# Ragged self-attention on one core: value products moved behind the last projection in four positions, counters raised ahead in the 256 loop, one score group in other banks

## The chip, the cores and the metric

The kernel runs on 1 core of one Trainium2 chip. The metric is the device time of one execution in microseconds (us), as the median of several runs. Its engines are TensorE (PE in the profile, PEld for its weight loads), VectorE (DVE), ScalarE (ACT), GpSimd (POOL) and SyncE (SP), which here issues nearly all DMAs.

## What is computed

Self-attention with 8 heads of 64 over 32 sequences of different lengths, without an output projection. The lengths are drawn once, between 64 and 511; rows beyond a sequence's length are zero in the output.

```python
for b in range(batch):
    x_b = x[b, :seq_len].copy()
    qkv = np.matmul(x_b, w_qkv)
    q, k, v = np.split(qkv, 3, axis=-1)
    ...
    scores = scale * np.matmul(q, k.transpose(0, 2, 1))
    attn = np.exp(scores - scores_max)
    attn = attn / (np.sum(attn, axis=-1, keepdims=True) + 1e-08)
    out_b = np.matmul(attn, v).transpose(1, 0, 2).reshape(seq_len, dim)
    output[b, :seq_len] = out_b
```

## The kernel before

**Loops and positions.** The kernel sorts the sequences by length on the chip and takes them in 16 pairs, longest first. There is one hardware loop for each width N in `LOOPS` (512, 448, 384, 352, 320, ... 96); a pair runs in the narrowest loop that holds its longer sequence. With this draw the last loops run as follows: 288 once, 256 once, 224 twice, 192 once, 160 twice, 128 once, 96 once. Each pass of a loop has two positions, j = 0 and j = 1. Position j computes the attention of the pair's sequence j, and between these steps the projections (queries, keys, values) of the sequence that comes next.

**The order of work** within a position is written out by hand as a string per loop, `ORDER`, one half for each position. A step is a letter and a number, and behind @ stand the PSUM banks (of 8) that it uses:

- `S` a group of scores, with its exponentials on ScalarE (line 1298). TensorE line 1280.
- `B`, `U`, `V..a` projections (queries and keys; values) made of 64-row matmuls in two or three parts a, b, c that share two banks (line 1334). Letters behind the colon tell which engine copies the banks out, d for VectorE and a for ScalarE.
- `Q`, `K`, `V` the same as full 128-row matmuls in one bank (lines 303 and 314); * means copied by ScalarE, else by VectorE.
- `A` value products: exponentials times values. `A0@3` is line 1528 with 128 rows (`av`); `A0a@23 ... A0b` come in two parts of 64 rows (`paired`, line 1642).
- `Z` the products with the last half tile of keys, 64 rows (`rest`, line 1568). In the loops where the last tile is at most half full (here 192 and 160, among others), the normalisation of two A steps follows only behind their Z.
- `W`, `E` smaller projection steps; `L`, `P` masks on VectorE and the cast of the next x on GpSimd.
- `D` and `X`: SyncE loads a later x, and transposes the cast x by DMA into `xT`, which the projections of the same position in the next pass read. X may only overwrite `xT` when the last projection of its position has read it.

**Normalisation.** Behind A (or Z), VectorE does three instructions for each A step: the row sums times a mask (`U`, line 1743, or 1704 for a paired A), the reciprocal (`R`, 1739 or 1695) and the division out of PSUM into the output tile (`O`, 1677). Only after `O` is the bank free. Each engine runs its instructions strictly in the order in which the steps stand. In P, VectorE's mask for the next cast stands behind the divisions of the position before.

**Waits.** `plan_waits` works out from the data and the banks which step waits for which; a wait is a semaphore against a counter register. These registers are raised once per pass (`raise_all`). On TensorE `LATE` says how many of its last steps of a pass stand behind the raising, with their waits corrected for it; the raising and the branch run on TensorE's sequencer while queued matmuls still run. Without an entry, the raising comes last.

**SyncE** goes through X, D and the store of the output (ST, once all `O` of the position are done) in that order, position by position.

The diff touches only `LATE` (line 41) and four entries of `ORDER` (lines 265 to 279), and with them what `position` (line 1038 on) emits in which order.

Of the kernel before, what the change touches and what calls it, by code (L numbers as in the profile page):

```python
# [18 lines left out]
P = 128  # L19
# [18 lines left out]
    passed: object = None  # L38


LATE = {288: 3, 224: 3, 192: 1, 160: 3}


def plan_waits(head, bodies, entries, rare):
# [136 lines left out]
def kernel(  # L181
# [9 lines left out]
    B, MAXS, D = x.shape  # L191
# [15 lines left out]
    def ring(n, shape, dtype, name, pool=const):  # L207
# [74 lines left out]
    }  # L282
# [1714 lines left out]
    for v, N in enumerate(LOOPS):  # L1997
        mine = [k for k, op in enumerate(bodies[v][1]) if op.eng == "PE"]
        tails_of.append(mine[len(mine) - LATE.get(N, 0) :])
        assert not any(bodies[v][1][k].skip for k in tails_of[v])  # L2000
# [242 lines left out]
```

## Time and profile before

| | us |
|---|---|
| median of 3 runs (lowest to highest) | 325.65 (325.38 to 325.74) |
| the profiled execution | 326.82 |
| its span, first to last instruction | 325.0 |
| TensorE busy in the span | 311.3 |
| ScalarE, VectorE, GpSimd busy | 264.0, 193.4, 100.6 |

The granted TensorE clock is 0.993 of full speed in the mean. The positions that the change touches lie in the last third of the span. By the starts of TensorE's first score group: 288 loop, position 0 at 209.80; 256 loop at 230.78, its position 1 at 237.99; 224 loop at 244.9 (with a projection); 192 loop at 272.98, position 1 at 278.46; 160 loop, first pass at 285.10 and 290.74, second pass at 296.49 and 301.37; 128 loop at 307.42.

How to read the lines: in a timeline a line is start in us, duration in us, engine, line of the program, operation, what is written and read, the shape, how many instructions were merged, and in brackets how long the engine was idle before it and what released it. TensorE's matmuls overlap and their ends are modelled, so the distance of two starts says more than a duration. In the chain of waits a line is start, duration and what the end of the span waited for.

### The profile page before, as it was taken

How to read it: one execution, taken by the hardware profiler on the slowest of the kernel's cores; microseconds unless marked ns; L12 is line 12 of the kernel's file. 1: busy time of each engine (PE TensorE's matmuls, PEld its weight loads, DVE VectorE, ACT ScalarE, POOL GpSimd, SP SyncE). 2: the span in 40 equal slices, each digit the busy share in tenths (PEclk: the TensorE clock that was granted, in tenths of full speed). 3: DMA queues.
4: the chain of work that ended last, by engine and by line, in shares of the span. 5: the costliest groups of instructions: out<-in, count | busy, mean ns of one | idle time of the engine just before them, and what ended most of it. 6: DMA issues, size and time to landing. Idle time of an engine off the chain costs nothing.

```text
span 325.0 us, 13310 instructions
## 1 busy us (share of the span) xinstructions
PE 311.3 (96%) x5092; PEld 202.2 (62%) x5092; DVE 193.4 (60%) x650; ACT 264.0 (81%) x415; POOL 100.6 (31%) x147
## 2 busy tenths in 40 slices
PE   7999999999999999999999999999999899999991
PEld 4444645555656556556556657657787787877861
DVE  6866566566665546456456456436575666666753
ACT  4489899797878988988988979898877678777761
POOL 2657040414030330330330342143222223533420
PEclk9999999999999999999999999999999999999997
DMA  6986858497848999597677777756459957896652
GB/s 216 373 316 72 259 180 277 94 351 171 281 50 281 224 294 261 185 285 226 227 225 226 244 210 198 221 169 219 135 150 206 233 179 178 180 239 161 216 180 81
DMA packets 69448, 68.85 MB, mean 212 GB/s; under 512 B 40720, under 2 KB 40720, under 8 KB 69392
## 3 DMA queue, kind: packets, MB, share of 16 engines
q1 hardware_dynamic: 69344, 68.12, 74.8%
q8 instruction: 33, 0.54, 0.7%
q14 instruction: 23, 0.19, 0.2%
q10 hardware_dynamic: 48, 0.00, 0.0%
HBM read 25.17 MB, written 33.55 MB: 181 GB/s over the span
## 4 chain that ended last, share of the span: by engine, by line
PE 88%; DMA 4%; DVE 2%; issue 1%; ACT 1%; SPq 1%; POOL 0%; POOLq 0%; DVEq 0%
PE banks L1334 43%; PE banks L1280 14%; PE banks L1528 12%; PE banks L314 7%; PE banks L303 6%; DMA xT<-x 3%; PE banks L1642 3%; PE banks L1221 1%; PE banks L1568 1%; DMA x_nat<-in_x_dram 1%; DVE out_nat L1677 0%; PE banks L768 0%; ACT et L1298 0%; SPq L331 0%; ACT xT L777 0%
## 5 line engine op out<-in xcount | busy, mean ns | idle before, releaser
L1298 ACT ACTIVATE et<-banks 128x704 f16<-128x704 f32 (+8 forms) x256 | 199.1, 825 | 25.8 <-PE banks L1280 22.0
L374 POOL TENSOR_TENSOR x<-x_nat,mask 128x512 f16<-128x512 f32 x82 | 83.1, 1039 | 177.1 <-DVE mask L1062 170.0
L1334 PE MATMUL banks<-xT,w_r 64*128 64x352 f16 (+9 forms) x1536 | 127.7, 294 | 1.4 <-DMA xT<-x 1.0
L1334 PEld LDWEIGHTS banks<-xT,w_r 64*128 64x128 f16 x1536 | 68.9, 94 | 37.8 <-PE banks L1334 8.7
L1280 PE MATMUL banks<-qz,kT 64*128 64x352 f16 (+11 forms) x624 | 77.4, 294 | 1.3 <-ACT et L1298 0.4
L1677 DVE SCALAR_TENSOR_TENSOR out_nat<-rcp,banks 128x256 f32<-128x256 f32 (+1 forms) x128 | 59.4, 470 | 6.5 <-DMA out_dram<-out_nat 2.2
L1378 DVE CAST qz<-banks 128x448 f16<-128x448 f32 (+6 forms) x47 | 26.4, 562 | 46.6 <-PE banks L1334 45.8
L1528 PEld LDWEIGHTS banks<-v_aug,et 128*128 128x128 f16 x1248 | 42.0, 97 | 14.4 <-issue 7.2
L1528 PE MATMUL banks<-v_aug,et 128*128 128x65 f16 x1248 | 47.6, 194 | 0.7 <-ACT et L1298 0.6
L1334 PE MATMUL banks<-w_r,xT 64*128 64x512 f16 (+1 forms) x368 | 46.6, 372 | 0.3 <-ACT v_aug L1500 0.3
L1280 PEld LDWEIGHTS banks<-qz,kT 64*128 64x128 f16 x624 | 28.0, 94 | 24.0 <-issue 5.9
L1743 DVE TENSOR_TENSOR rcp<-banks,queries 128x4 f32<-128x4 f32 (+1 forms) x110 | 17.3, 157 | 19.8 <-PE banks L1528 7.3
L1397 DVE CAST v_aug<-banks 128x512 f16<-128x512 f32 x25 | 16.6, 690 | 19.2 <-PE banks L1334 19.2
L314 PE MATMUL banks<-w_r,xT 128*128 128x512 f16 x104 | 26.7, 380 | 0.0
L1334 PEld LDWEIGHTS banks<-w_r,xT 64*128 64x128 f16 x368 | 17.1, 94 | 14.5 <-PE banks L1334 1.0
L303 PE MATMUL banks<-xT,w_r 128*128 128x160 f16 (+3 forms) x256 | 23.2, 243 | 1.1 <-issue 0.6
L1378 ACT CAST kT<-banks 128x352 f16<-128x352 f32 (+6 forms) x47 | 22.5, 479 | 1.5 <-PE banks L1334 1.5
L1739 DVE RECIPROCAL rcp<-rcp 128x4 f32<-128x4 f32 (+1 forms) x110 | 20.2, 184 | 3.8
L1378 DVE CAST kT<-banks 128x352 f16<-128x352 f32 (+5 forms) x33 | 17.9, 552 | 7.7 <-PE banks L1334 7.6
L303 PEld LDWEIGHTS banks<-xT,w_r 128*128 128x128 f16 x256 | 16.5, 98 | 6.2 <-issue 1.2
L1378 ACT CAST qz<-banks 128x352 f16<-128x352 f32 (+6 forms) x33 | 15.3, 464 | 3.4 <-PE banks L1334 3.3
L1500 ACT CAST v_aug<-banks 128x512 f16<-128x512 f32 x15 | 8.9, 590 | 9.5 <-PE banks L314 9.5
(117 smaller groups left out, 180.4 us busy)
## 6 DMA issues: line engine op xcount, KB each, us to landing
x_nat<-in_x_dram SPq DMA_DIRECT2D x12, 768.0 KB, 6.7
out_dram<-out_nat SPq DMA_DIRECT2D x12, 768.0 KB, 4.1
x_nat<-in_x_dram SPq DMA_DIRECT2D x14, 512.0 KB, 4.6
out_dram<-zeros SPq DMA_DIRECT2D x12, 512.0 KB, 3.7
out_dram<-out_nat SPq DMA_DIRECT2D x12, 512.0 KB, 5.1
out_dram<-out_nat SPq DMA_DIRECT2D x4, 1024.0 KB, 6.8
x_nat<-in_x_dram SPq DMA_DIRECT2D x3, 1024.0 KB, 7.0
out_dram<-zeros SPq DMA_DIRECT2D x4, 768.0 KB, 4.5
```

The source lines that it names most:

```text
L303: last = nc.tensor.matmul(dst[:, 0:N], w_r[:, c, w0 : w0 + P], xT[:, c, 0:N], start=(c == 0), stop=(c == NC - 1),)
L314: last = nc.tensor.matmul(pv, xT[:, c, t * P : (t + 1) * P], w_r[:, c, 2 * D : 3 * D], start=(c == 0), stop=(c == NC - 1),)
L374: return engine.tensor_tensor(out=x16, in0=x32, in1=live.broadcast_to([P, D]), op=ALU.mult)
L1280: last = nc.tensor.matmul(psc[par][:, x * wide : x * wide + N], kT[r, i, c0 : c0 + P], qz[r, i, 0:N], start=True, stop=True,)
L1298: return nc.scalar.activation(out=et[:, :, x0:x1, 0:N], in_=got.rearrange("p j (x q) -> p j x q", q=wide)[:, :, x0:x1, 0:N], func=AF.Exp, ...
L1334: last = nc.tensor.matmul(to, lhs(rows, c), rhs(rows, c), start=(c == 0 and opens), stop=(c == NC - 1 and not opens),)
L1378: return lambda copy, bank: copy(out=buf[:, ms, 0:M], in_=bank[:, 0 : gm * M].rearrange("p (m q) -> p m q", q=M),)
L1397: return lambda copy, bank: copy(out=v_bufs[o][:, t, :, 0:HD], in_=bank.rearrange("p (h d) -> p h d", d=HD))
L1528: last = nc.tensor.matmul(pav[:, g, qt, :], e_bufs[e][:, c0 + qt * P : c0 + (qt + 1) * P], v_aug[:, kt, h, :], start=(kt == 0 and not (hal ...
L1677: return nc.vector.scalar_tensor_tensor(out=o_t[:, 0:n, h0 * HD : (h0 + heads) * HD].rearrange("p t (g d) -> p t g d", d=HD), in0=by, scal ...
L1739: return nc.vector.reciprocal(out=r, in_=total if n == 1 else r)
L1743: return nc.vector.tensor_tensor(out=r.rearrange("p (t g) -> p t g", t=n), in0=total.rearrange("p (t g) -> p t g", t=n), in1=rows, op=ALU. ...
```

## The change

- **288, position 0:** the score group S3 uses banks 6 and 7 instead of 5 and 6.
- **256, position 1:** A0b and B1b change places, and A4 and A6 move from ahead of B1c, the last projection part, to the end. `LATE` gets an entry 256: 2, so TensorE raises its counters ahead of these two.
- **192, position 1:** V0a moves ahead of A1a, and A1b from ahead of V0b to the end. `LATE` was 1 and stays 1, so the step behind the raising is now A1b instead of V0b.
- **160, both positions:** A2 and Z0 move behind the last projection (Q2 in position 0, V0 in position 1), to stand ahead of A4, A6 and Z4.

X and D keep their place among SyncE's steps; they now stand ahead of the moved value products in the string. The number of instructions of each kind stays the same.

```diff
-LATE = {288: 3, 224: 3, 192: 1, 160: 3}
+LATE = {288: 3, 256: 2, 224: 3, 192: 1, 160: 3}
...
-        288: "L P D S0@56 B2a@24 S5@01 B2b:aa S3@56 B0a@01 S1@23 S9@45 B0b:dd S2@67 B1a@32 S6@45 B1b:da S4@67 "
+        288: "L P D S0@56 B2a@24 S5@01 B2b:aa S3@67 B0a@01 S1@23 S9@45 B0b:dd S2@67 B1a@32 S6@45 B1b:da S4@67 "
...
         256: "L P S0@34 U0a@02 S1@56 U0b:aa B0a@17 S2@34 S3@56 B0b A0a@02 B0c:da B1a@34 A0b B1b A1a@67 B1c:ad X D "
-        "A1b | L P S0@01 U0a@25 S1@34 U0b:ad B0a@76 S2@01 E0@4 B0b A0a@23 B0c:da B1a@45 S3@01 A0b B1b A4@6 "
-        "A6@7 B1c:aa X D",
+        "A1b | L P S0@01 U0a@25 S1@34 U0b:ad B0a@76 S2@01 E0@4 B0b A0a@23 B0c:da B1a@45 S3@01 B1b A0b B1c:aa "
+        "X D A4@6 A6@7",
...
         192: "L P S0@01 S1@23 V0*@5 B0a@40 S3@67 B0b A0a@53 S2@12 A0b B1a@67 B0c:aa B1b A1a@21 B1c:ad X D A1b | L "
-        "P B0a@50 S1@34 B0b S2@67 B0c:da W0@4 S0@12 B1a@03 S3@67 E0@5 B1b A0a@12 B1c:aa A0b A1a@46 V0a@57 A1b "
-        "V0b:aa X D",
-        160: "L P S0@01 S1@23 V0@5 Q0*@4 A0@0 K0*@7 A2@1 S2@23 Z0 K2*@6 Q2*@7 X D A4@5 A6@2 Z4 | L P S0@34 S1@67 "
-        "K2@0 Q2*@1 A0@3 W0*@4 Q0@6 A2@5 K0*@0 Z0 S2@12 V0*@6 X D A4@4 A6@7 Z4",
+        "P B0a@50 S1@34 B0b S2@67 B0c:da W0@4 S0@12 B1a@03 S3@67 E0@5 B1b A0a@12 B1c:aa A0b V0a@57 A1a@46 "
+        "V0b:aa X D A1b",
+        160: "L P S0@01 S1@23 V0@5 Q0*@4 A0@0 K0*@7 S2@23 K2*@6 Q2*@7 X D A2@1 Z0 A4@5 A6@2 Z4 | L P S0@34 S1@67 "
+        "K2@0 Q2*@1 A0@3 W0*@4 Q0@6 K0*@0 S2@12 V0*@6 X D A2@5 Z0 A4@4 A6@7 Z4",
```

The unchanged entries of the two loops that follow are needed to see who uses which bank next: 224 begins `L P B0a@30 S0@12`, and 128 begins `L P S0@12 Q0*@6 K0*@0 V0@7`.

## The prediction

> **What bounds the kernel now.** I read the page first, for who ends the span, then the timeline of TensorE around the five changed positions, then VectorE, ScalarE and SyncE at those places, and the chain of waits.
>
> ```profile
> PE 88%; DMA 4%; DVE 2%; issue 1%; ACT 1%; SPq 1%; POOL 0%; POOLq 0%; DVEq 0%
> ```
>
> TensorE carries 88% of the chain that ended last. So an edit pays only where it closes a gap in TensorE's row, and costs where it opens one. I call the four runs of the 160 loop P0 (first pass, position 0), P1 (first pass, position 1), P2 and P3 (second pass); the 128 loop follows.
>
> ```profile
> 287.08 0.29 PE L1528 MATMUL banks<-v_aug,et 128*128 128x65 f16 x4
> 287.20 0.71 PE L303 MATMUL banks<-xT,w_r 128*128 128x160 f16 x8
> 287.76 0.28 PE L1528 MATMUL banks<-v_aug,et 128*128 128x65 f16 x4
> 287.97 0.31 PE L1280 MATMUL banks<-qz,kT 64*128 64x160 f16 x4
> 288.12 0.28 PE L1568 MATMUL banks<-v_aug,et 64*128 64x65 f16 x8
> 288.34 1.07 PE L303 MATMUL banks<-xT,w_r 128*128 128x160 f16 x13
> 290.06 0.37 PE L303 MATMUL banks<-xT,w_r 128*128 128x160 f16 x3 [0.65 <-issue]
> ...
> 290.74 0.58 PE L1280 MATMUL banks<-qz,kT 64*128 64x160 f16 x12
> 291.26 1.28 PE L303 MATMUL banks<-xT,w_r 128*128 128x160 f16 x16
> 292.38 0.29 PE L1528 MATMUL banks<-v_aug,et 128*128 128x65 f16 x4
> ...
> 294.05 0.72 PE L303 MATMUL banks<-xT,w_r 128*128 128x160 f16 x8
> 294.70 0.30 PE L1568 MATMUL banks<-v_aug,et 64*128 64x65 f16 x8
> 294.83 0.30 PE L1280 MATMUL banks<-qz,kT 64*128 64x160 f16 x4
> ...
> 295.94 0.41 PE L1528 MATMUL banks<-v_aug,et 128*128 128x65 f16 x8
> ...
> 296.49 0.62 PE L1280 MATMUL banks<-qz,kT 64*128 64x160 f16 x12
> 297.09 1.04 PE L314 MATMUL banks<-w_r,xT 128*128 128x512 f16 x4
> ...
> 306.57 0.41 PE L1528 MATMUL banks<-v_aug,et 128*128 128x65 f16 x8
> 306.92 0.30 PE L1568 MATMUL banks<-v_aug,et 64*128 64x65 f16 x8
> 307.42 0.40 PE L1280 MATMUL banks<-qz,kT 64*128 64x128 f16 x8 [0.20 <-ACT v_aug L1500]
> ...
> 309.54 1.03 PE L314 MATMUL banks<-w_r,xT 128*128 128x512 f16 x4
> ...
> 311.63 1.53 PE L303 MATMUL banks<-xT,w_r 128*128 128x96 f16 x32 [0.48 <-DMA xT<-x]
> ```
>
> Starts tell more than durations here, since the ends are modelled. In P0, A0 (287.08, four matmuls) is followed by 128-row work and takes 0.12 us from start to start; A2 (287.76), the same four matmuls, takes 0.21 because the 64-row S2 follows. So a change between 128-row and 64-row matmuls costs 0.09 us. A half product Z0 takes 0.13 where 64-row work follows (294.70 to 294.83) and 0.22 where it doesn't (288.12 to 288.34): the same 0.09.
>
> ```profile
> 292.18 0.42 DVE L1677 SCALAR_TENSOR_TENSOR out_nat<-rcp,banks 128x256 f32<-128x256 f32 x1
> ...
> 292.81 0.48 DVE L1453 CAST kT<-banks 128x320 f16<-128x320 f32 x1
> ...
> 295.04 0.16 DVE L1743 TENSOR_TENSOR rcp<-banks,queries 128x4 f32<-128x4 f32 x1 [0.42 <-PE banks L1568]
> ...
> 295.87 0.42 DVE L1677 SCALAR_TENSOR_TENSOR out_nat<-rcp,banks 128x256 f32<-128x256 f32 x1 [0.46 <-DMA out_dram<-out_nat]
> 296.21 0.15 DVE L1743 TENSOR_TENSOR rcp<-banks,queries 128x4 f32<-128x4 f32 x1
> ...
> 296.61 0.42 DVE L1677 SCALAR_TENSOR_TENSOR out_nat<-rcp,banks 128x256 f32<-128x256 f32 x1
> ```
>
> This is VectorE behind P0 and P1. P1's four divisions start only after Z0: the first link of the chain begins at 295.04, 0.21 after Z0's work. A link that isn't held up takes 0.82 from its begin to the end of its division (296.21 to 297.03), and divisions follow 0.74 apart (295.87, 296.61). These divisions release PSUM banks. The second, O2, holds bank 5 and ends at 297.03; the next position's V0@5 starts at 297.09. That is no accident: P2's V0 waits for it already.
>
> **The change, part by part.** *160.* A2 and Z0 go behind the last projection in all four runs. That removes no work. It adds two row changes per run (Z0 now lies between 128-row products), 0.19 us, and starts the division chain later, while the next position wants the banks as early as before.
>
> P0: the gap before 290.06 has no releaser, so I take it for code arriving. It comes after 65 matmuls of the loop; in the new order these end inside Z0. The work before it stays nearly the same, so I keep its end at 290.06. Three matmuls of Z0 (0.05), a row change, A4 and A6 (0.25, twice four as above), another change and Z4 (0.13) end P0 at 290.67, 0.07 before 290.74. Bound: with the gap gone altogether, 0.6 less.
>
> P1: P0's Z0 ends at 290.11, the chain begins at 290.32, O0 ends 291.14, O2 291.88, O6 293.36. K2@0 needs O0's bank and comes at 291.19, just in time. Q2@1 comes 0.56 later (half of 291.26 to 292.38) and needs O2: it waits 0.18, to 291.94. K2's copy, behind O6 on VectorE, ended 0.69 after it (293.29 against 292.60), so now at 294.05; K0@0 needs that bank, comes at 294.04 (294.05 − 0.07 + 0.18 − 0.12 for A2) and waits 0.06. With the row changes P2 starts 0.36 late (0.19 + 0.24 − 0.07), at 296.85.
>
> P2: P1's V0 no longer has A2 and Z0 ahead, so it ends at 295.94 + 0.17 − 0.25 = 295.86, and Z0 behind A2 and a row change at 296.20. The chain begins at 296.41: O0 ends 297.23, O2 297.97. S1@23, 0.21 behind S0, needs bank 3 from O0 and waits 0.2, to 297.29. V0@5 then comes at 297.59 and waits for O2 until 298.03. It started at 297.09, so P2 is 0.94 late at V0, and 1.13 at its end.
>
> P3: P1's waits recur (0.24), with two row changes, so Z4, which ended at 307.05 (306.92 and 0.13), ends at 307.05 + 1.56 = 308.61. Here the change pays: the 128 loop's first scores started at 307.42, 0.37 behind Z4, because they wait for ScalarE's copy of V0, 0.85 behind V0's end at 306.57. V0 now ends at 306.57 + 1.13 + 0.24 − 0.25 = 307.69, so the scores start at about 308.65, 1.23 late. V0@7 of the 128 loop would come at 309.54 + 1.23 = 310.77, but P3's last division holds bank 7: Z0 ends 308.03, the chain begins 308.24 and its fourth division ends 3.04 later, 311.28. V0@7 waits 0.57 and is 1.80 late. Then the 0.48 of wait for transposed x at 311.63 falls away: 1.32 late.
>
> ```profile
> 291.58 3.97 SPq L331 DMA_TRANSPOSE xT<-x  x2
> ...
> 297.99 1.26 SPq L331 DMA_TRANSPOSE xT<-x  x1
> ```
> ```profile
> 306.86 4.51 DMA xT<-x
> ```
>
> Are the transposes sooner, as the order allows? P0's last projection ended three matmuls behind 290.06 and P1's at 295.94, but SyncE reached their transposes at 291.58 and 297.99: its own queue of loads and stores holds them, not TensorE. P3's, at 306.86, does follow its projection; that now ends at 307.69, so it goes out at 308.0, and with the old 4.51 it lands at 312.5, before its reader at 312.95. SyncE's store behind P3 waits for the late O6 (311.28) and holds back the 128 loop's own transpose; its reader has moved 1.3 too, so I price that from 0 to 0.3 and take 0.1. GpSimd's casts wait for a mask that VectorE makes behind the divisions; they move along, hidden as long as SyncE comes later still.
>
> The row change is weighed once more. The rows say 0.09 each. The Trainium skill ("TensorE: Matmul & The Clock Gate", Part 3, the mechanism) says that a weight load to other rows, or to the background buffer, is pulled ahead of running matmuls, by which a change would be free and the sum 0.3 less; the trace speaks against that here.
>
> *256.*
>
> ```profile
> 242.79 0.41 PE L1642 MATMUL banks<-v_aug,et 64*128 64x65 f16 x16
> ...
> 244.48 1.05 PE L1334 MATMUL banks<-xT,w_r 64*128 64x224 f16 x16
> ...
> 252.82 0.56 PE L1334 MATMUL banks<-xT,w_r 64*128 64x224 f16 x8 [0.96 <-DMA xT<-x]
> ```
> ```profile
> 243.68 0.75 DVE L1677 SCALAR_TENSOR_TENSOR out_nat<-rcp,banks 128x256 f32<-128x256 f32 x2
> ```
> ```profile
> 246.43 6.25 DMA xT<-x
> ```
>
> A4 and A6 go behind the last projection part, A0b behind B1b, about 0.8 later (sixteen matmuls, as many as the row at 244.48). A0b's division ended at 244.43; it will end at 245.2, and the next loop's first projection, the second half of that row and so due at 244.9, needs its bank: 0.3 late. Raising the counters ahead hides a loop end that can't be longer than a small part of that row. Both lie ahead of the 0.96 of wait at 252.82, which swallows them. What counts is when that transpose lands. It goes out some 0.6 earlier, but it took 6.25 on the chain against 4.51 above, so it stands in the queue. I take its landing as unchanged, 0; ends 0.6 earlier and 0.1 later.
>
> *192 and 288.*
>
> ```profile
> 284.46 0.61 PE L1334 MATMUL banks<-w_r,xT 64*128 64x256 f16 x8
> 285.10 0.62 PE L1280 MATMUL banks<-qz,kT 64*128 64x160 f16 x12
> ```
> ```profile
> 212.99 0.30 PE L1280 MATMUL banks<-qz,kT 64*128 64x288 f16 x2 [0.36 <-ACT et L1298]
> ```
> ```profile
> 212.25 2.95 ACT L1298 ACTIVATE et<-banks 128x576 f16<-128x576 f32 x5
> ```
>
> In 192, V0a moves ahead of A1a, and A1b goes last. A short stall ahead of V0b can close, since A1a's sixteen products now cover V0a's drain where A1b's eight did. But V0b's start (284.46) lies 0.64 before the next loop (285.10), 0.2 more than its eight matmuls fill, so TensorE already waits there for the branch; the branch comes behind A1b now, a third as long a cover. What the one gives the other takes: 0, ends −0.1 and +0.1. In 288, S3 leaves bank 5, so S9@45 waits no longer for S3's exponential but for a copy that ends before it. The 0.36 goes, yet ScalarE's five exponentials run without a break and the second is awaited soon after. I take 0.15 off; ends 0 and 0.36.
>
> **Sum.** 1.32 + 0.1 − 0.15 = 1.27 on a profiled execution of 326.82 us (span 325.0): 328.1. That execution lies 1.17 above the median of 325.65, so the forecast is 326.9.
>
> **Rivals.** *Transposes win (faster).* If the later divisions hold nobody up, because the waits in the 160 loop ask for an earlier count than I read, P1 to P3 cost only row changes (0.5 at Z4, with P0's gain); the 0.37 before 307.42 pays most of that, and the wait at 311.63 the rest. If then the 256 transpose lands 0.6 earlier and 288 gives 0.15, the kernel is 0.75 faster: 324.9. It decides at P2's V0, which must start without a wait for VectorE. Against it: V0 starts 0.06 behind O2 in the trace. *Offset (no change).* The gap in P0 goes (−0.6) and the 256 transpose lands 0.6 earlier, with the chain as forecast: +0.07, 325.7. *The gap grows.* Code arrives 0.6 later in P0: 327.5.
>
> **How the numbers follow.** About 0.65 us (0.2%) is what can be told from no change. Chances: forecast within its bounds 0.66, gap grows 0.06, offset 0.16, transposes win 0.12. The forecast's own range is 326.2 to 327.4. The range for 8 in 10 adds the larger gap and most of the offset case: 325.4 to 327.6.
>
> **What would show it.** Right: two more row changes in each run of 160; P2's S1 and V0 and the 128 loop's V0 waiting for VectorE's divisions; the waits at 307.42 and 311.63 gone; the start at 252.82 within 0.2. Wrong: P2 as long as before, or the start at 252.82 moved by 0.5.

## The result, and the profile after

The changed kernel takes 329.02 us in the median of nine runs (327.86 to 329.93), the kernel before 326.0 (325.38 to 328.08). The ratio is 1.0082, with a 95% interval of 1.0059 to 1.0105: 1.9 to 3.4 us slower, 2.7 by the ratio itself. The forecast was 1.27 slower, so the sign was right and the size was less than half; the time lies above the range given for 8 in 10 (325.4 to 327.6). The profiled execution of the changed kernel took 329.93, with a span of 328.1.

By engine, the chain that ended last in the changed kernel:

```profile
PE 87%; DVE 5%; issue 2%; DMA 2%; ACT 1%; SPq 1%; POOL 0%; DVEq 0%; POOLq 0%
```

VectorE has gone from 2% to 5%: its divisions now stand on the path. TensorE's timeline in the 160 loop and behind it, changed kernel (P0's end, the start of P2, then the 128 loop):

```profile
289.85 1.28 PE L303 MATMUL banks<-xT,w_r 128*128 128x160 f16 x16
290.96 0.29 PE L1528 MATMUL banks<-v_aug,et 128*128 128x65 f16 x4
291.18 0.30 PE L1568 MATMUL banks<-v_aug,et 64*128 64x65 f16 x8
291.41 0.42 PE L1528 MATMUL banks<-v_aug,et 128*128 128x65 f16 x8
...
298.06 0.86 PE L1280 MATMUL banks<-qz,kT 64*128 64x160 f16 x12
299.29 1.04 PE L314 MATMUL banks<-w_r,xT 128*128 128x512 f16 x4 [0.36 <-DVE out_nat L1677]
...
310.01 0.40 PE L1280 MATMUL banks<-qz,kT 64*128 64x128 f16 x8
310.34 1.96 PE L303 MATMUL banks<-xT,w_r 128*128 128x128 f16 x32
312.73 1.02 PE L314 MATMUL banks<-w_r,xT 128*128 128x512 f16 x4 [0.43 <-DVE out_nat L1677]
313.59 0.42 PE L1528 MATMUL banks<-v_aug,et 128*128 128x65 f16 x8
313.95 0.40 PE L1280 MATMUL banks<-qz,kT 64*128 64x128 f16 x8
314.81 0.38 PE L303 MATMUL banks<-xT,w_r 128*128 128x96 f16 x5 [0.46 <-DVE v_aug L1500]
```

The order is the one described: projections (289.85), then A2, Z0, A4 and A6. The wait ahead of the 128 loop's first scores, at 307.42 before, is gone at 310.01, as forecast. P2's V0 (299.29) now starts 1.23 behind its first scores (298.06) and names VectorE's division as releaser; before, the distance was 0.60. The 128 loop's V0 (312.73) waits for the same line. The last row is the one to remember: 0.86 lie between the scores and the projection behind them, as before (310.76 to 311.63 there), but the releaser is another one. VectorE at that place, changed kernel:

```profile
309.54 0.16 DVE L1743 TENSOR_TENSOR rcp<-banks,queries 128x4 f32<-128x4 f32 x1 [1.69 <-PE banks L1568]
...
312.17 0.42 DVE L1677 SCALAR_TENSOR_TENSOR out_nat<-rcp,banks 128x256 f32<-128x256 f32 x1
...
313.80 0.69 DVE L1500 CAST v_aug<-banks 128x512 f16<-128x512 f32 x1 [0.33 <-PE banks L314]
```

P3's four divisions run from 309.54 to 312.59, 3.05 (forecast 3.04). V0 starts 0.14 after that, and its copy out of bank 7 ends at 314.49, 0.32 before the projection starts. In the kernel before, VectorE's same copy:

```profile
310.61 0.69 DVE L1500 CAST v_aug<-banks 128x512 f16<-128x512 f32 x1 [0.91 <-PE banks L314]
```

It ended at 311.30, 0.33 before 311.63; the transposed x landed at 311.37 (306.86 and 4.51). Two waits ended 0.07 apart, and the view named only the later.

**Stages.** TensorE's matmuls have the same count in both kernels, so the distance from the start of one stage to the start of the next can be compared. In us, for four profiled executions of the kernel before and three of the changed one (the first of each is the one shown; the others are told below):

| stage | before | changed | forecast |
|---|---|---|---|
| head, first to 65th matmul | 10.30, 10.45, 10.46, 10.11 | 11.74, 11.18, 10.37 | 0 |
| 288, position 0 | 10.60, 10.58, 10.58, 10.58 | 10.39, 10.38, 10.38 | -0.15 |
| 256, position 1 | 6.99, 6.98, 7.00, 6.98 | 7.29, 7.28, 7.28 | +0.3 |
| 224, to the row at 252.82 | 7.85, 7.74, 7.89, 6.81 | 7.22, 7.21, 7.21 | -0.3 |
| 192, position 1 | 6.64, 6.36, 6.35, 6.12 | 7.25, 6.97, 7.25 | 0 |
| P0 | 5.64, 5.65, 4.84, 5.37 | 5.05, 5.05, 5.05 | -0.07 |
| P1 | 5.74, 5.74, 5.87, 5.75 | 6.16, 6.16, 6.16 | +0.43 |
| P2 | 4.88, 4.83, 4.87, 4.83 | 5.72, 5.73, 5.72 | +0.77 |
| P3 | 6.05, 6.05, 6.05, 6.05 | 6.23, 6.23, 6.23 | +0.10 |
| 128, position 0 | 3.34, 3.34, 3.34, 3.34 | 3.94, 3.94, 3.94 | +0.57 |
| 128, scores to projection | 0.88, 0.86, 0.86, 0.88 | 0.86, 0.95, 0.95 | -0.48 |
| from there to the last matmul | 7.31, 7.30, 7.30, 7.30 | 7.29, 7.29, 7.29 | +0.1 |

The rows from P1 on repeat within 0.13 in these seven executions. From P2 on they are properties of the order; P1 is so only where its transposed x is there in time, which it was not in five other kernels with the 160 loop's old order (told at the 256 edit). The head, the 224 and 192 loops and P0 differ between executions of one and the same kernel.

And the 256 loop's follower. First VectorE in the kernel before (the last division of 256, the copy of the 224 loop's queries), then TensorE and VectorE in the changed one:

```profile
245.49 0.42 DVE L1677 SCALAR_TENSOR_TENSOR out_nat<-rcp,banks 128x256 f32<-128x256 f32 x1
...
247.74 0.62 DVE L1378 CAST qz<-banks 128x448 f16<-128x448 f32 x1 [0.43 <-PE banks L1334]
```
```profile
246.32 0.56 PE L1334 MATMUL banks<-xT,w_r 64*128 64x224 f16 x8 [0.32 <-DVE out_nat L1677]
...
250.25 1.04 PE L1334 MATMUL banks<-w_r,xT 64*128 64x512 f16 x8 [0.45 <-DVE qz L1378]
...
253.54 0.55 PE L1334 MATMUL banks<-xT,w_r 64*128 64x224 f16 x8
```
```profile
247.32 0.42 DVE L1677 SCALAR_TENSOR_TENSOR out_nat<-rcp,banks 128x256 f32<-128x256 f32 x1
...
249.57 0.62 DVE L1378 CAST qz<-banks 128x448 f16<-128x448 f32 x1 [0.43 <-issue]
```

The 0.32 at 246.32 is the forecast 0.3. But there is a second wait, at 250.25, for a copy on VectorE that starts 2.25 behind the last division in both kernels (245.49 to 247.74, 247.32 to 249.57). The last division starts 1.00 behind the 224 loop's first projection (246.32) where it was 0.52 (245.49 against 244.97), so the copy is 0.48 late. And the wait for the transposed x, which stood at 252.82, is gone at 253.54.

### The profile page after: what moved, and what is told of

It reads as the page before. It is cut to its first block, busy times and chain, and to the rows that moved or that the text cites. A ratio compares the mean times of both kernels' runs of the same rounds, so it can differ in the third digit from the quotient of the medians.

```text
span 328.1 us, 13312 instructions
## 1 busy us (share of the span) xinstructions
PE 312.4 (95%) x5092; PEld 201.8 (62%) x5092; DVE 193.5 (59%) x650; ACT 263.6 (80%) x415; POOL 100.7 (31%) x147
## 4 chain that ended last, share of the span: by engine, by line
PE 87%; DVE 5%; issue 2%; DMA 2%; ACT 1%; SPq 1%; POOL 0%; DVEq 0%; POOLq 0%
PE banks L1334 43%; PE banks L1280 13%; PE banks L1528 12%; PE banks L314 7%; PE banks L303 6%; PE banks L1642 3%; DVE out_nat L1677 2%; DMA x_nat<-in_x_dram 2%; PE banks L1221 1%; PE banks L1568 1%; DVE rcp L1739 1%; ACT et L1298 1%; DVE v_aug L1500 0%; SPq L645 0%; DVE rcp L1743 0%
```

## The experiments

Theory A: VectorE's late divisions hold banks, and behind waits that seemed to fall away others stand. Its rivals: B, gaps that shift with the position of the code; C, the 256, 192 and 288 edits.

**One group of edits at a time.** Only the 160 loop's two orders are taken from the change:

```diff
-... K0*@7 A2@1 S2@23 Z0 K2*@6 Q2*@7 X D A4@5 ... A2@5 K0*@0 Z0 S2@12 V0*@6 X D A4@4 ...
+... K0*@7 S2@23 K2*@6 Q2*@7 X D A2@1 Z0 A4@5 ... K0*@0 S2@12 V0*@6 X D A2@5 Z0 A4@4 ...
```

> Only the two orders of the 160 loop are changed. Theory A (late divisions of the 160 loop hold PSUM banks, and a second wait, for VectorE's copy of V0 in the 128 loop, stands behind the wait for transposed x): this run carries the loss, +1.4 from the 160 loop and its follower and +0.5 from that second wait, so +1.9 us (+0.6%); P2 about 0.85 longer, the 128 loop's position 0 about 0.6 longer, its position 1 not shorter. Theory B (gaps of code fetch that shift with the layout, in the head and in the first passes of the loops, make up half of the loss): +1.0 to +1.5, and the start of the 288 loop as in the kernel before or shifted without regard to this edit. Theory C (the 256, 192 and 288 edits carry the rest of the loss): +1.4.

328.26 (six runs) against 325.88; ratio 1.0083 (1.0055 to 1.0112). P0 5.05, P1 6.22, P2 5.67, P3 6.23, the 128 loop 3.93 and 0.86: every stage of the changed kernel. Its total is as much slower as the whole change; its 288 loop starts at 209.77, as before.

Only the 256 loop's order and its entry in `LATE`:

> Only the 256 loop's position 1 and its entry in LATE are changed. Theory A: 0 to -0.6 us; position 1 of 256 is 0.3 longer, the wait for transposed x in the 224 loop at 252.82 swallows it, and the transpose lands up to 1 us earlier. Theory B: a new gap of 0.4 us in the 224 loop behind that place, and the sum within 0.3 of zero. Theory C: +0.3 to +0.7.

326.72 (twelve runs); ratio 1.0034 (1.0009 to 1.0060). Position 1 is 7.29, the stretch behind it 7.21. The stretch after that is 7.31 against 7.18, so B's gap of 0.4 is not there. The interval, 0.3 to 2.0 us, lies above A's. One reason is that the cover that A counted on (the wait at 252.82) is not always there, as is shown below. Another stands in this run's profiled execution (328.71): P1, which no edit touches, took 7.22, with a wait that neither the kernel before nor the changed one showed:

```profile
292.97 1.27 PE L303 MATMUL banks<-xT,w_r 128*128 128x160 f16 x16 [1.42 <-DMA xT<-x]
```

The same wait is in the profiled executions of four other kernels that leave the 160 loop as it was (192 alone 0.58, the runs with other banks in the 128 loop 1.37 and 0.40, the first of those that take the 256 edit apart 1.20). It comes and goes like the others, and what it adds to the timed medians is not known.

Only the 192 loop's position 1:

> Only the order of position 1 of the 192 loop is changed. Theory A: within 0.15 us of the kernel before. Theory B: the gap inside A0a, which has no releaser, grows from 0.5 to 1.2 us, so +0.7. Theory C: +0.5 to +0.7 as well, but in the steps that were moved (V0a, A1a, V0b, A1b).

326.23 (twelve runs); ratio 1.0008 (0.9991 to 1.0025), position 1 at 6.40. No cost of the edit can be told, as A says.

All but the 160 loop's:

> The edits of 288, 256 and 192 together, with the 160 loop as before. Theory A: -0.15 to -0.75 us. Theory B: +0.5 to +1.0, with the loss in gaps without a releaser and in the head, ahead of the 288 loop. Theory C: +1.0 to +1.3, in the changed positions.

325.96 (twelve runs); ratio 1.0005 (0.9979 to 1.0030). Together the three make no difference that these runs could tell. A's gain isn't there either: 288 wins 0.2 (10.39), and 256's position 1 loses 0.3 (7.29).

**One position of 160 at a time.** A2 and Z0 moved in position 0 alone, then in position 1 alone:

> In the 160 loop A2 and Z0 are moved in position 0 alone (P0 and P2); read from TensorE's starts by stage, since one look can't tell 0.5 us in the total. The chain theory (late divisions hold the banks of the position that follows): P1 and P3 are 0.2 to 0.45 longer than unedited, P2 is 0.2 longer (row changes alone, without its waits for O0 and O2), and the 128 loop's position 0 stays at 3.34. Rival (what costs is what the moved order itself does to TensorE: row changes and the fetch of code at another place): P0 and P2 carry the loss, P2 +0.8, P1 and P3 nothing.

> The same for position 1 alone (P1 and P3). The chain theory: P1 and P3 gain or lose at most 0.2, P2 is 0.65 longer (S1 waits 0.2 to 0.3, V0 0.4), and the 128 loop's position 0 is 0.6 longer. Rival (the moved order itself): P1 and P3 carry the loss, P2 stays at 4.83 and the 128 loop's position 0 at 3.34.

| kernel | P0 | P1 | P2 | P3 | 128, position 0 | scores to projection |
|---|---|---|---|---|---|---|
| position 0 alone | 5.05 | 5.92 | 5.05 | 6.22 | 3.34 | 0.86 |
| position 1 alone | 4.84 | 5.91 | 5.51 | 5.99 | 3.93 | 0.86 |

(326.49 and 328.00 us, one execution each.) The loss lies in the position that follows the moved one, as A says. Position 1 alone makes P2 0.68 longer, with nothing changed in P2 itself, and the 128 loop 0.59. Position 0 alone costs P0 and P2 the 0.2 of the row changes, and the positions that follow, P1 and P3, 0.17 and 0.18. TensorE at P2 with position 1 alone moved:

```profile
296.43 0.87 PE L1280 MATMUL banks<-qz,kT 64*128 64x160 f16 x12
297.65 1.04 PE L314 MATMUL banks<-w_r,xT 128*128 128x512 f16 x4 [0.36 <-DVE out_nat L1677]
```

**Other banks for the changed order.** If banks are the cause, other banks must cure it without moving a step.

```diff
-... A0@3 W0*@4 Q0@6 K0*@0 S2@12 V0*@6 X D A2@5 Z0 A4@4 A6@7 Z4
+... A0@5 W0*@4 Q0@3 K0*@0 S2@12 V0*@3 X D A2@4 Z0 A4@7 A6@6 Z4
-        128: "L P S0@12 Q0*@6 K0*@0 V0@7 X D A0@6 A4@5 | L P S0@23 E0@7 ...
+        128: "L P S0@12 Q0*@3 K0*@0 V0@5 X D A0@6 A4@7 | L P S0@23 E0@0 ...
```

> The changed kernel with other banks in position 1 of the 160 loop and in the 128 loop, so that a step that comes soon finds a bank that an early division frees; nothing else is moved. The chain theory: P2 falls from 5.72 to 5.05 (the row changes stay), P1 and P3 keep their 0.24 and may wait 0.1 more at A0; the 128 loop's position 0 falls from 3.94 to 3.4, and in its position 1 the 0.86 from the scores to the projection falls to 0.4, if nothing but VectorE's copy of V0 held it: together 1.6 us less than the changed kernel, +0.3% to +0.4% against the kernel before. Rival (row changes and code): P2 stays at 5.7, the total at +0.8%.

P2 fell to 5.03 and the last 0.86 to 0.33, as A says. But the kernel took 331.54 (four runs), ratio 1.0142 (1.0079 to 1.0206): the 128 loop's position 0 took 7.29. TensorE and the clock there:

```profile
308.41 0.40 PE L1280 MATMUL banks<-qz,kT 64*128 64x128 f16 x8
311.05 3.17 PE L303 MATMUL banks<-xT,w_r 128*128 128x128 f16 x32 [2.24 <-DVE out_nat L1677]
```
```profile
311.05:311.60 0.55, 0.55 (x10) 0.55 (x11) 0.20 (x2) 0.00 (x0) 0.00 (x0) 0.96 0.84 317
311.60:314.00 2.40, 2.40 (x26) 2.40 (x24) 0.27 (x2) 0.59 (x1) 1.04 (x1) 0.50 0.60 230
```

Q0 in bank 3 waits 2.24 for P3's last division. Bank 3 was freed long before, but in the 128 loop's own second pass its holder would be that loop's A0, whose division, as the plan in the kernel reads, carries the same counter as the last one of the 160 loop, and the plan asks for that. The stretches (start and end, length, busy time of PE, PEld, DVE, ACT and POOL, granted clock, DMA share, GB/s) show what came on top: the clock fell to 0.50. A second set avoids it, with the 160 loop as in the first:

```diff
+        128: "L P S0@12 Q0*@0 K0*@5 V0@7 X D A0@6 A4@0 | L P S0@23 E0@5 ...
```

> The changed kernel with other banks in position 1 of the 160 loop and in the 128 loop, this time so that no step of the 128 loop waits for the last division: Q0 takes bank 0, K0 bank 5 (freed by the first division), V0 stays in 7 (freed by the third), E0 goes to 5, so that it doesn't wait for the copy of V0. The chain theory: P2 5.05 instead of 5.72, the 128 loop's position 0 3.35 instead of 3.94, and 0.35 to 0.5 instead of 0.86 from its second scores to the projection: some 1.7 us less than the changed kernel, so +0.3% against the kernel before (what is left: row changes, P1's and P3's 0.24, and the 256 loop's 0.8). Rival (row changes and code): P2 and the 128 loop's position 0 as in the changed kernel, +0.8%.

> The kernel with the second set of banks once more. If its loss behind the 128 loop is its own (SyncE's transpose for the 96 loop, which waits behind the store of the late division, takes the place of the waits that the banks removed): the 96 loop's first projection waits 0.3 to 1.7 for transposed x again. If it was chance: no wait there, and a total near 328.

In two executions (the second took 330.00) P2 is 5.02 and 5.03, the 128 loop's position 0 3.35 in both, and the scores to the projection 0.58 and 0.48. TensorE at P2 and at the 128 loop's V0, without a wait at either:

```profile
297.36 0.59 PE L1280 MATMUL banks<-qz,kT 64*128 64x160 f16 x12
297.88 1.04 PE L314 MATMUL banks<-w_r,xT 128*128 128x512 f16 x4
...
309.12 1.96 PE L303 MATMUL banks<-xT,w_r 128*128 128x128 f16 x32
310.92 1.03 PE L314 MATMUL banks<-w_r,xT 128*128 128x512 f16 x4
```

So the banks are the cause of these waits; that is shown, and row changes and code as their cause have fallen. The total, however, is 330.97 (five runs), ratio 1.0142 (1.0111 to 1.0173), far from the +0.3% expected. The second of these executions at the 96 loop, and its clock:

```profile
316.84 1.67 PE L303 MATMUL banks<-xT,w_r 128*128 128x96 f16 x32 [1.96 <-DMA xT<-x]
318.30 1.91 PE L314 MATMUL banks<-w_r,xT 128*128 128x512 f16 x4
```
```profile
314.50:316.80 2.30, 0.35 (x8) 0.22 (x8) 1.27 (x5) 1.44 (x3) 0.23 (x2) 1.00 0.32 118
316.80:318.30 1.50, 1.46 (x32) 1.47 (x33) 0.00 (x0) 0.48 (x1) 0.20 (x1) 0.93 0.46 175
318.30:320.00 1.70, 1.70 (x7) 0.60 (x5) 0.00 (x0) 0.48 (x1) 0.00 (x0) 0.50 0.00 0
```

The 96 loop's first projection waits for transposed x, 1.66 in the first and 1.96 in the second; the changed kernel has no wait there. From the 128 loop's second projection to the last matmul it is 8.81 and 10.48 where the changed kernel takes 7.29. (The other banks also cost 0.28 in P0 and 0.2 each in P1 and P3.) Part of it follows from the chain: the transpose goes out 2.25 behind P3's last division, as in the changed kernel (311.37 to 313.62, 312.59 to 314.83), while TensorE is earlier. The rest is that it took 2.6 and 2.9 from the end of its issue to its landing, against 1.1 in the changed kernel. A 16 KiB code fetch ran into both of these and not into that one; that it is the reason is argued only.

**The second wait by itself.** In the kernel before, three banks of the 128 loop are changed so that E0 needn't wait for VectorE's copy of V0, first alone and then with 288's score group as in the change:

```diff
-        128: "L P S0@12 Q0*@6 K0*@0 V0@7 X D A0@6 A4@5 | L P S0@23 E0@7 ...
+        128: "L P S0@12 Q0*@6 K0*@0 V0@5 X D A0@6 A4@7 | L P S0@23 E0@0 ...
```

> The kernel before with three banks of the 128 loop changed (V0 in 5, A4 in 7, E0 in 0), so that E0 no longer waits for VectorE's copy of V0 out of bank 7. If that copy is the wait that ends last at the place where the prediction let 0.48 fall away: the 0.86 from the scores to the projection falls to 0.4 to 0.5, and the kernel gains 0.3 to 0.46 us (-0.1%). If the transposed x is the last, it stays above 0.8 and nothing is gained.

> The kernel before with two edits: the score group of 288 in banks 6 and 7, as in the change, and the three banks of the 128 loop (V0 in 5, A4 in 7, E0 in 0). By the stages seen so far 0.2 in the 288 loop and 0.37 in the 128 loop: 0.55 us faster than the kernel before (-0.17%). If the 128 loop's later steps give it back, -0.06%.

The 0.86 fell to 0.49 and 0.35. TensorE in the second of the two:

```profile
308.84 0.40 PE L1280 MATMUL banks<-qz,kT 64*128 64x128 f16 x8
309.19 1.53 PE L303 MATMUL banks<-xT,w_r 128*128 128x96 f16 x32
```

So the copy held it, in executions in which the transposed x is there in time (in the first of the two, TensorE's weight load still waited 0.3 for the transposed x). The totals can't be told from the kernel before: 326.86 (ten runs, 1.0014, 0.9974 to 1.0053), and with 288's edit 325.61 (twelve runs, 0.9989, 0.9968 to 1.0010). What lies behind gives 0.18 back in the latter (7.48 against 7.30).

**The 256 edit taken apart.** First A4 and A6 behind the last projection, with early counters, but A0b ahead of B1b as before; then the whole new order with the counters raised last:

> The kernel before with A4 and A6 of the 256 loop behind the last projection and the early counters, but A0b left ahead of B1b; read by stages. Theory A (VectorE's queue of divisions: the later A0b delays its division, whose bank the 224 loop asks first, and all that stands behind it on VectorE, a mask and the copy of Q0): the first of the two losses goes, position 1 stays at 6.98, and the stretch from the 224 loop's first projection to its next one is 6.7 to 6.9 instead of 7.2, since A6's division moves by only 0.2 to 0.4. Rival (the early counters cost it): position 1 stays at 7.28 and the stretch at 7.2.

> The kernel before with the new order of the 256 loop, but without its entry in LATE: the counters are raised last. Read by stages. If the loss of the 256 edit is VectorE's later queue alone and the early counters neither cost nor gain: position 1 stays at 7.28 (7.0 to the end of A6, then 0.3 until the bank), since the 0.3 that the first projection of the 224 loop waits for VectorE's division covers the raising and the branch; the stretch that follows stays at 7.2. If the early counters earn something: more than 7.28 by what they earn. If they cost it: 7.0.

(328.64 and 326.47 us, one execution each; in the first, the 192 loop's position 1 took 7.46 and P1 7.00, which the edit doesn't touch.) Without the early counters, position 1 is 7.28 and the stretch 7.21: by these stages they do nothing. With A0b early, position 1 is 7.12, but the stretch is 7.22 still, so A's division of the loss failed. VectorE there:

```profile
246.53 0.42 DVE L1677 SCALAR_TENSOR_TENSOR out_nat<-rcp,banks 128x256 f32<-128x256 f32 x1
...
248.78 0.62 DVE L1378 CAST qz<-banks 128x448 f16<-128x448 f32 x1 [0.43 <-issue]
```

The last division starts 1.01 behind the loop's first projection (245.52), as in the changed kernel: it follows A6, not A0b. The second loss (0.48) comes with A4 and A6, of the first (0.3) half comes with A0b.

**The two kernels again.** Both unchanged, for what repeats (the kernel before took 326.66, 325.96 and 324.81, the changed one 329.08 and 328.84):

> The kernel before once more, for what differs from look to look: by the runs so far the stretch from the 224 loop's first projection to the one that waited 0.96 is 6.73 to 7.4 and not 7.85, P0 4.84 and not 5.64, and the 0.86 from the 128 loop's second scores to the projection is the same with VectorE's copy named as the releaser.

> The changed kernel once more. What is a property of the order recurs within 0.05: 288's position 0 10.37, 256's position 1 7.29, the stretch behind it 7.22, P0 5.05, P1 6.2, P2 5.72, P3 6.22, the 128 loop's position 0 3.94 and 0.86. What was chance doesn't: the 1.44 more at the head, 7.60 in the 224 loop, 7.25 in the 192 loop.

> The kernel before, a third look. If the gap of 0.8 in P0 and the long stretch ahead of 252.82 belong to this program: P0 5.64 and 7.7 to 7.9 again, at a time near 326.7. If they are draws of single executions: a look nearer to the median of 325.9 lacks one of them (P0 4.84, or a stretch of 6.7 to 7.4).

> The kernel before, a fourth look. As in the third: P0 5.64 and a stretch of 7.7 to 7.9 if these belong to the program, P0 4.84 or a stretch of 6.7 to 7.4 if they are draws.

> The changed kernel, a third look. If the longer head (11.2 to 11.7 until the 64th matmul) and the longer 192 loop (7.0 to 7.25) belong to the program, they come again; if they are draws, the head is anywhere from 10.0 to 11.7 and the 192 loop's position 1 from 6.2 to 7.4, as over all the runs so far. The stages of 256, 160 and 128 recur within 0.05.

The stages stand in the table above. The second profile of the kernel before names VectorE's copy at the place where the first named the DMA:

```profile
311.23 1.53 PE L303 MATMUL banks<-xT,w_r 128*128 128x96 f16 x32 [0.46 <-DVE v_aug L1500]
```

The third has no gap in P0 (sixteen projections in one row), but the long wait in the 224 loop; the fourth has neither that wait nor the whole gap, and is the fastest:

```profile
252.90 0.56 PE L1334 MATMUL banks<-xT,w_r 64*128 64x224 f16 x8 [1.00 <-DMA xT<-x]
...
288.16 1.28 PE L303 MATMUL banks<-xT,w_r 128*128 128x160 f16 x16
```
```profile
251.56 0.56 PE L1334 MATMUL banks<-xT,w_r 64*128 64x224 f16 x8
...
288.03 0.37 PE L303 MATMUL banks<-xT,w_r 128*128 128x160 f16 x3 [0.35 <-issue]
```

## Why the prediction was right in its chain and wrong in its size

**Right, and shown.** The chain from Z0 over the divisions to the next position's banks: P1 longer by 0.4 (forecast 0.43; its first projections take 1.31 where they took 1.12, by the forecast wait of 0.18), P2 by 0.87 (0.77), P3 by 0.18 (0.10), the 128 loop's position 0 by 0.60 (0.57). The banks were tried by themselves, and P2 and the 128 loop obeyed. The price of a row change holds too: P0 without a gap goes from 4.84 to 5.05, 0.21 for two. 288 gave 0.20 for 0.15, and of 192 no cost could be told.

**Wrong: "Then the 0.48 of wait for transposed x at 311.63 falls away: 1.32 late."** This is the step that failed in the sum. The distance stayed 0.86 to 0.95: 0.05 more in the mean instead of 0.48 less, so 0.53 of what the forecast lacked. Behind the DMA, 0.07 earlier, VectorE's copy of V0 released bank 7 for E0; it follows V0, which the change itself delays. The copy and its 0.69 were in VectorE's rows. The prediction asked what is late next for most waits, and not here.

**Wrong: "Both lie ahead of the 0.96 of wait at 252.82, which swallows them."** The 0.3 came as forecast, with 0.48 more from VectorE's copy, which stands behind the late divisions. The wait that should swallow them was 1.00 in one execution and absent in another of the same kernel. Where it is long, the edit gains: the transposes go out 0.77 ahead of the 224 loop's first projection instead of 0.21 behind it (245.55 and 246.32; 245.18 and 244.97), and the stretch is 7.21 instead of 7.8. Where it is absent, the edit costs 0.3 and up to 0.48 (6.73 was the shortest stretch without it, in two kernels). So the prediction's sign, the start at 252.82, decides nothing: counted from the start of the 256 loop, the changed kernel's first execution is there 0.45 earlier than the one shown of the kernel before (21.59 and 22.04) and 0.64 later than its fourth (20.95).

**Wrong: P0's end kept at 290.06.** The gap there is not always present (P0 took 5.64, 5.65, 4.84 and 5.37), and the changed kernel showed none in three executions. Against a run without it, P0 costs 0.21, not -0.07. Its place was read rightly: the kernel with the first other banks, whose position 0 is the changed one, has the gap inside Z0, behind the 64th matmul of the loop, where the prediction had put it:

```profile
289.40 0.23 PE L1568 MATMUL banks<-v_aug,et 64*128 64x65 f16 x4
289.96 0.24 PE L1568 MATMUL banks<-v_aug,et 64*128 64x65 f16 x4 [0.32 <-issue]
```

The last two have one root. The prediction noted that its profiled execution lay 1.17 above the median, and subtracted that as if it were spread evenly. The other executions suggest that it lay in just those gaps on which it leaned: the wait is up to 1.0 us and the gap 0.8, and the fourth execution, without the one and with part of the other, took 324.81.

**The account.** Against the mean of the four executions, the stages from P1 to the 128 loop's second projection cost 0.39 + 0.87 + 0.18 + 0.60 + 0.05 = 2.1. P0 gives 0.3, 288 gives 0.2, 256 with its follower gives 0.1 (0.3 against 0.36, and 0.08 in its position 0): some 1.4 in all. That this is near the forecast of 1.27 is luck: the 0.53 that the wait at 311.63 was mis-sized by (0.05 for -0.48) is made up in the main by P0 and 256, whose gains hang on a gap and a wait that come and go. The profiled executions differ by 3.2 in the mean. The rest lies in the head (0.8), in the 192 loop's position 1 (0.8) and in small parts of the 224 loop. The head is a matter of chance: the third execution of the changed kernel has 10.37. The 192 loop's position was 7.0 to 7.25 three times in the changed kernel and 6.1 to 6.6 four times in the other; but with its edit alone it was 6.40, in the kernel with the second set of banks 7.42 and 6.22, and in three kernels with the old order of 192 it was 7.11, 7.18 and 7.46, so the edit doesn't make it. It also trades places with the gap in P0: in all nine profiled executions in which the 192 position took 6.90 or more, P0 shows no gap, so P0's 0.3 is not the change's own gain either. What the timed 2.7 has beyond the 1.4 stays open: gaps in 192, and waits for transposed x such as P1's, are candidates, and no run here shows how often they come in the one kernel and in the other. For the 160 edit alone, 2.1 and P0's 0.2 lie inside the timed interval (1.8 to 3.6 us).

## What to carry to other kernels

When a forecast lets a wait "fall away", list every wait of that instruction and when each ended, not only the one that the profile names: two that end 0.07 us apart are one obstacle. And before a wait or a gap is counted as cover, see it in a second execution: what makes one execution slower than the median may be the cover itself. Late work on an engine that isn't the bottleneck costs in the next stage, through the buffers that it releases and through what queues behind it there.

## What the runs showed of the hardware

The granted clock fell to 0.50 behind a wait of 2.24 us, from 0.55 us after the matmuls had begun again, and in another kernel behind one of 1.96 (0.93 for 1.5 us, then 0.50 for 1.7); behind one of 1.66 it stayed at 1.00. The Trainium skill ("TensorE: Matmul & The Clock Gate", Part 1, What's actually happening) puts the fall at an idle window of about 3.4 us. These runs show it behind shorter waits. In the first case the 128 loop's position 0 took 7.29 instead of 3.35, and only 2.24 of the 3.94 are the wait: the slow matmuls cost nearly as much again.

TensorE's gaps without a releaser in the first pass of a loop differ between executions of one program: P0's was 0.8 in two, 0.5 in a third and none in a fourth, by the length of P0; the 192 loop's position 1 took 7.42 and 6.22. The Trainium skill ("Runtime: NRT & Kernel Launch", Instruction fetch mechanics) calls the price of crossing a block of code mostly hidden; it was not hidden here in every execution, if these gaps are that. The DMA records of the traces speak for it: in the five profiled executions with a gap in P0, TensorE went on 1.27 to 1.44 behind the end of a 16 KiB code fetch, always at the 65th or 66th matmul of the loop, and in all but one of the fifteen without one that matmul came later behind it, 1.5 to 3.0. No run moved a fetch, so it is not proven.
